# Two-direction recurrence beside conditioning products: later rank, a fourth weight tile, four column groups, and a substitution by halves

## Chip, core and metric

One NeuronCore of one Trainium2 chip runs the whole program in one launch. The metric is device microseconds (us) of that core; lower is better. Engines: PE (TensorE, matmuls), DVE (VectorE), ACT (ScalarE), POOL (GpSimd), SP (issues DMAs).

## What is computed

Two blocks, one after the other, on 512 tokens and 256 context tokens of width 1024. Block 1 mixes a two-direction RWKV recurrence with latent attention; block 2 has four attention layers. Each of the layers of both blocks is conditioned on a vector:

```python
mod   = silu(c)     @ ada_w[i] + ada_b[i]      # 1024 -> 3072, shift, scale, gate
mod_c = silu(c_ctx) @ ada_w[i] + ada_b[i]

def step(S, inp):                               # forward, and once more with reverse=True
    r_t, w_t, k_t, v_t, a_t, b_t = inp
    sa = einsum('bhij,bhj->bhi', S, a_t)
    S = S * w_t[..] + sa[..., None] * b_t[..] + v_t[..., None] * k_t[..]
    return S, einsum('bhij,bhj->bhi', S, r_t)
```

The four conditioning products of block 2 depend on nothing that block 1 computes.

## The kernel before

Block 1 does its projections and attention first (to about 480 us of the span). Then `rwkv` runs the recurrence in chunks of 64 tokens, two chunks to a **unit**, six units for each direction (d = 0 forward, d = 1 backward). For a unit, `rw_prep` builds the chunk matrices on all engines, and `rw_inv` inverts a triangular 64x64 matrix for each head and chunk. That goes through 16x16 diagonal blocks: they are carried to another layout by DMA through DRAM (tiles `dd`), solved on DVE by substitution (L1733 to L1735, 15 steps of one product and one reduction over all the columns before it, once for both directions), carried back, and put together to 64x64 with 32x32 matmuls (line L1750, tile `psi`). Then `rw_step` takes the state through two chunks (PE lines L1825 to L1848, tiles `psc`, `pss`), and adds to the result `y` (L1855). After the recurrence, `gnorm(0)` normalises the first pair of token tiles (PE L1540, DVE L1544 to L1577), the product with `w_out` follows, then `gnorm(1)`.

Beside the recurrence stands a generator, `fillers`. It emits the conditioning products of block 2, which `rwkv` draws a few pieces at a time (`self.fills`). `ada_steps` computes them: 4 layers x 3 thirds of 1024 columns; a third takes 16 weight tiles `adw` (128x512 f32, 256 KB each, loaded by L234 on the SP queue), each multiplied (L237) into the one PSUM tile `pad`; then the bias (L231, L240), the evacuation to an `adw` tile (L242, DVE) and stores to `mods` (L252). That is 192 weight tiles. The tiles `adw` come round robin out of a few buffers, so a load waits until the matmul that read the buffer last is through. `self.adj` is the number of column groups J: the 1024 columns of a third lie as J rows of 1024/J columns at partitions 0, 32, ... of `pad`, so one matmul has 1024/J columns and column group j of the array:

```python
nc.tensor.matmul(p[32 * j:32 * j + 32, 0:n], lhsT=sT[:, k, :], rhs=wt[:, c0:c0 + n], ...,
                 tile_position=(0, 32 * j))
```

Block 1's own conditioning at the start of the program (psw, 128x256) already has J = 4.

A scheduler sets the order of every engine's instructions at build time: by a rank, which is the place in the program unless `high_priority` moves it, and by its own estimate of when operands are there. An engine, and the DMA queue on SP, then takes its instructions strictly in that order. Unit 0's preparation and all of `rw_step` have high priority; the other pieces stand at their places.

Of the kernel before, what the change touches and what calls it, by code (L numbers as in the profile page):

```python
# [11 lines left out]
F32 = mybir.dt.float32  # L12
# [4 lines left out]
ALU = mybir.AluOpType  # L17
AX = mybir.AxisListType
# [1058 lines left out]
class Block1(Block2):  # L1077
# [371 lines left out]
    def rwkv(self, rp, adp):  # L1449
        nc, a = self.nc, self.a  # L1450
        big = [128, 4, 2, 128]
        self.slots(rp, [(f"{n}{q}", big, 2, F32) for q in range(2) for n in ("bt", "mb", "xa", "xb")])
        self.w2 = rp.tile([128, 512], F32, name="w2")
        self.a2 = rp.tile([128, 512], F32, name="a2")
        self.w0 = rp.tile([128, 2, 512], F32, name="w0")
        self.slots(rp, [("e", [128, 512], self.ebufs, F32), ("P", [128, 4, 2, 65], 2, F32), ("bk", big, 2, F32)])
        self.slots(rp, [("iv", [128, 16, 16], 3, F32)])
        for d in range(2):
            self.slots(rp, [(f"ih{d}", [128, 8, 32], 2, F32), (f"dg{d}", [128, 8, 16], 2, F32)])

        self.zd = [[rp.tile([128, 8, 32], F32, name=f"zd{d}{i}") for i in range(3)] for d in range(2)]
        for d in range(2):
            for t in self.zd[d]:
                nc.gpsimd.memset(t, 0.0)
        nc.sync.dma_start(out=self.w2, in_=a["rw_w2"][0].rearrange("d e f -> (d e) f"))
        nc.sync.dma_start(out=self.a2, in_=a["rw_a2"][0].rearrange("d e f -> (d e) f"))
        nc.sync.dma_start(out=self.w0, in_=a["rw_w0"][0].unsqueeze(0).to_broadcast([128, 2, 512]))
        nc.scalar.activation(out=self.wi, in_=self.wi, func=AF.Tanh)
        self.ha0 = rp.tile([128, 8], F32, name="ha0")
        nc.vector.tensor_scalar(self.ha0, self.a0c, 0.5, None, op0=ALU.mult)  # L1470
        self.hka = rp.tile([128, 2, 4], F32, name="hka")
        nc.vector.tensor_scalar(self.hka[:, 0], self.kac, 0.5, None, op0=ALU.mult)
        nc.vector.tensor_scalar(self.hka[:, 1], self.kac, -0.5, 1.0, op0=ALU.mult, op1=ALU.add)

        self.i32 = rp.tile([128, 32], F32, name="i32")
        nc.vector.tensor_reduce(out=self.i32, in_=self.ident.rearrange("p (b t) -> p t b", t=32), axis=AX.X, op=ALU.add)

        gl = self.gl
        for i, v in enumerate((a["rw_lnx_g"][0], a["rw_lnx_b"][0])):
            for h in range(2):  # L1480
                nc.sync.dma_start(out=gl[64 - 64 * h:128 - 64 * h, i], in_=v.rearrange("(a h v) -> h a v", h=2, v=64)[h].unsqueeze(0).to_broadcast([64, 4, 64]))
        nc.vector.tensor_scalar(gl, gl, 0.5, None, op0=ALU.mult)
        self.Rn = [None, None]
        self.psum(3, (("ad", 1), ("w", 3), ("c0", 1), ("c1", 1), ("iv0", 1), ("iv1", 1)))
        fill = iter(())
        if self.second:
            fill = self.fillers(adp)
        for i in range(6):
            us = [None, None]
            gens = [self.rw_prep(rp, i, d, us) for d in range(2)]  # L1490
            r = 0
            while gens:
                with self.tc.high_priority() if i < self.early_units else ExitStack():
                    gens = [g for g in gens if next(g, self) is not self]
                r += 1
                for _ in range(self.fills[i]):
                    next(fill, None)
            with self.tc.high_priority():
                for s in range(2):
                    for d in range(2):  # L1500
                        self.rw_step(rp, i, d, s, us[d])
        for _ in fill:
            pass

    early_units = 1

    def fillers(self, adp):

        b = self.second
        self.adj = 2  # L1510
        sT = self.ada_cond(adp, b["c"], b["c_ctx"], "ad")
        self.mds = []
        g = self.rpb_rows(adp, b["b_rpb"][0], ("adw", 3), "ad")
        self.rpb = next(g)
        yield from g
        for l in range(4):
            g = self.ada_steps(adp, sT, b["ada_w"][l], b["ada_b"][l], ("adw", 3), "ad")
            self.mds.append(next(g))
            yield from g

# [176 lines left out]
    def rw_inv(self, rp, d, mb):  # L1697


        nc = self.nc  # L1700
# [23 lines left out]
        U, Z, tmp = self.sub  # L1724
# [5 lines left out]
        yield  # L1730
        if d == 1:
            nc.vector.tensor_copy(U[hs], tmp[hs].rearrange("p s t -> p t s"))
            for n in range(1, 16):  # L1733
                nc.vector.tensor_tensor(out=tmp[:, 0:n, 0:n], in0=Z[:, 0:n, 0:n], in1=U[:, 0:n, n].unsqueeze(1).to_broadcast([128, n, n]), op=ALU.mult)
                nc.vector.tensor_reduce(out=Z[:, 0:n, n], in_=tmp[:, 0:n, 0:n], axis=AX.X, op=ALU.add)  # L1735
            nc.vector.tensor_copy(tmp, Z.rearrange("p s t -> p t s"))
        yield
        for k, src, dst, q in ((2, (tmp, Z)[d][hs], zt, nc.scalar), (1, (Z, tmp)[d][hs], zd, nc.sync)):
# [5 lines left out]
        def wp():  # L1744
            return self.ps.tile([128, 8, 32], F32, tag=f"iv{d}", bufs=1, name="psi")
# [8 lines left out]
        p = wp()  # L1754
# [4 lines left out]
        p = wp()  # L1759
# [7 lines left out]
        p = wp()  # L1767
# [10 lines left out]
        p = wp()  # L1778
# [6 lines left out]
        p = wp()  # L1785
# [203 lines left out]
```

## Time and profile before

| | |
|---|---|
| median of 3 runs | 3094.74 us (3083.89 to 3104.61) |
| profiled run: time, span of its execution | 3110.49 us, 3108.7 us |
| PE, DVE, ACT, POOL busy over the span | 90%, 58%, 44%, 40% |
| recurrence with conditioning beside it | about 480 to 1022 us of the span |

Times of rows are us from the start of the span; a group's mean is in ns. A matmul of f32 leaves two records, so "x2" on L237 is one matmul; a few records are missing. PEclk is the granted share of the 2.4 GHz clock: 1.00 is 2.4 GHz, 0.50 is 1.2 GHz, and what lies between is a mean over a stretch. SPq rows are DMA issues on SP's queue. A busy PE is one with a matmul in flight, not one at its peak.

### The profile page before, as it was taken

To read this page: it belongs to the slowest core of one execution; us is meant where nothing else is said; L and a number is where in the kernel's file an instruction comes from. 1 tells how busy PE (TensorE), PEld (TensorE's weight loads), DVE (VectorE), ACT (ScalarE), POOL (GpSimd) and SP (SyncE) were. 2 spreads that over 40 slices of the span, in tenths; PEclk is the share of its full clock that TensorE was granted. 3 is DMA by queue.
4 is the path that set the end of the run, shared out by engine and by line. 5 is a ranking of instruction groups with operands and counts; after the bars stand their busy time and mean duration, and the time that the engine had idled before them with its cause. 6 is when DMAs were issued, how large, how long until landed. Compare 5 with 4: busy or idle time off the path is not lost.

```text
span 3108.7 us, 56171 instructions
## 1 busy us (share of the span) xinstructions
PE 2800.7 (90%) x21983; PEld 2409.1 (77%) x21983; DVE 1789.0 (58%) x3470; ACT 1364.3 (44%) x2940; POOL 1256.5 (40%) x1348
## 2 busy tenths in 40 slices
PE   6989987999999689998969999996999898789998
PEld 4978875555645688987969999886999797778878
DVE  3345534655454745667554655545677787556785
ACT  3435523322221344557434555534445354345673
POOL 3313344443321452534534554562432344334454
PEclk8999996998778689999989999998999999899999
DMA  5252144444344331011122111223111121221112
GB/s 186 59 157 73 51 138 127 118 118 115 93 115 123 126 94 42 28 39 45 44 88 63 52 45 54 65 81 89 55 38 32 42 66 53 62 80 57 48 35 72
DMA packets 252692, 238.40 MB, mean 77 GB/s; under 512 B 59218, under 2 KB 217859, under 8 KB 252427
## 3 DMA queue, kind: packets, MB, share of 16 engines
q1 hardware_dynamic: 217712, 217.48, 23.9%
q10 hardware_dynamic: 33770, 16.29, 1.8%
q8 instruction: 173, 2.83, 0.4%
q0 software_dynamic: 944, 1.05, 0.2%
q14 instruction: 93, 0.75, 0.1%
HBM read 207.15 MB, written 28.07 MB: 76 GB/s over the span
## 4 chain that ended last, share of the span: by engine, by line
PE 66%; DVE 16%; DMA 6%; issue 4%; ACT 4%; POOL 2%; SPq 0%; ACTq 0%; DVEq 0%; POOLq 0%
PE psw L187 10%; PE psw L188 10%; PE psw L189 10%; PE psp L567 5%; PE pad L237 4%; PE psi L1750 3%; PE ps L544 3%; PE ps L545 2%; PE pso L559 2%; PE psp L187 2%; PE psp L189 2%; PE psp L188 2%; PE psw L1659 2%; DMA gbc<-mods 1%; DMA adw<-in_ada_w_dram 1%
## 5 line engine op out<-in xcount | busy, mean ns | idle before, releaser
L180 POOL TENSOR_TENSOR wl<-wr,wh 128x512 fp32r<-128x512 f32 x362 | 481.8, 1346 | 556.3 <-ACT wh L373 442.4
L187 PE MATMUL psw<-wh,hh 128*128 128x256 f32 x2152 | 625.4, 291 | 43.0 <-DVE yt L697 33.7
L189 PE MATMUL psw<-wh,hl 128*128 128x256 f32 x2152 | 615.3, 286 | 1.9 <-POOL hl L180 1.8
L188 PE MATMUL psw<-wl,hh 128*128 128x256 f32 x2152 | 616.2, 286 | 0.3 <-POOL wl L180 0.3
L187 PEld LDWEIGHTS psw<-wh,hh 128*128 128x128 f32 x2152 | 413.6, 192 | 54.5 <-DVE yt L697 36.8
L189 PEld LDWEIGHTS psw<-wh,hl 128*128 128x128 f32 x2152 | 413.6, 192 | 2.9 <-POOL hl L180 2.7
L188 PEld LDWEIGHTS psw<-wl,hh 128*128 128x128 f32 x2152 | 414.0, 192 | 0.8 <-POOL wl L180 0.5
L527 DVE TENSOR_REDUCE nm<-ps 128x1 f32<-128x768 f32 (+2 forms) x384 | 293.3, 774 | 153.5 <-PE ps L545 122.0
L373 ACT CAST wh<-wr 128x512 fp32r<-128x512 f32 x362 | 221.7, 617 | 269.5 <-PE psw L189 123.0
L528 ACT ACTIVATE P<-ps,nm 128x768 f32<-128x768 f32 (+1 forms) x288 | 247.0, 859 | 170.9 <-DVE nm L527 151.9
L535 DVE TENSOR_TENSOR ptl<-psp,pth 128x512 fp32r<-128x512 f32 x360 | 244.1, 685 | 131.9 <-ACT pth L534 129.6
L534 ACT CAST pth<-psp 128x512 fp32r<-128x512 f32 x360 | 207.3, 588 | 145.0 <-PE psp L567 118.2
L187 PE MATMUL psw<-hh,wh 128*128 128x512 f32 (+1 forms) x640 | 230.6, 360 | 21.5 <-DVE z L405 15.4
L567 PE MATMUL psp<-ident,P 128*128 128x128 f32 x1408 | 219.3, 274 | 7.8 <-DVE P L1023 6.9
L188 PE MATMUL psw<-hl,wh 128*128 128x512 f32 (+1 forms) x640 | 225.9, 353 | 0.0
L189 PE MATMUL psw<-hh,wl 128*128 128x512 f32 (+1 forms) x640 | 225.7, 353 | 0.2 <-POOL wl L180 0.2
L544 PE MATMUL ps<-kh,qs 128*128 128x512 f32 (+1 forms) x608 | 203.6, 341 | 17.9 <-ACT P L528 11.3
L237 PE MATMUL pad<-adw,ad_s 128*32 128x512 f32 x384 | 200.6, 700 | 14.8 <-DMA adw<-in_ada_w_dram 11.3
L545 PE MATMUL ps<-kz,qs 128*128 128x512 f32 (+1 forms) x608 | 183.3, 320 | 0.0
L567 PEld LDWEIGHTS psp<-ident,P 128*128 128x128 f32 x1408 | 164.8, 141 | 10.6 <-DVE P L1023 6.8
L187 PEld LDWEIGHTS psw<-hh,wh 128*128 128x128 f32 x640 | 121.8, 190 | 42.3 <-DVE z L405 19.5
L183 POOL TENSOR_SCALAR u<-ot 64x512 f32<-64x512 f32 x88 | 50.9, 578 | 252.9 <-ACT ot L585 249.4
(490 smaller groups left out, 6307.0 us busy)
## 6 DMA issues: line engine op xcount, KB each, us to landing
adw<-in_ada_w_dram SPq DMA_DIRECT2D x240, 256.0 KB
wr<-in_a_w_in_dram SPq DMA_DIRECT2D x80, 256.0 KB
wr<-in_b_w_in_dram SPq DMA_DIRECT2D x64, 256.0 KB
wr<-in_c_w_in_dram SPq DMA_DIRECT2D x64, 256.0 KB
wr<-in_w_in_dram SPq DMA_DIRECT2D x52, 256.0 KB
gbc<-mods SPq DMA_DIRECT2D x72, 128.0 KB
xscr<-xt SPq DMA_DIRECT2D x36, 256.0 KB
wr<-in_a_w_out_dram SPq DMA_DIRECT2D x32, 256.0 KB
```

What stands on the lines that cost most here:

```text
L180: self.nc.gpsimd.tensor_tensor(out=out, in0=in0, in1=in1, op=op)
L187: mm(out, lhsT=ah, rhs=bh, start=start, stop=False)
L188: mm(out, lhsT=ah, rhs=bl, start=False, stop=False)
L189: mm(out, lhsT=al, rhs=bh, start=False, stop=stop)
L237: nc.tensor.matmul(p[32 * j:32 * j + 32, 0:n], lhsT=sT[:, k, :], rhs=wt[:, c0:c0 + n], start=(k == 0), stop=False, tile_position=(0, 32 * j))
L373: nc.scalar.copy(out=h, in_=raw)
L527: nc.vector.tensor_reduce(out=nm, in_=S, axis=AX.X, op=ALU.max, negate=True)
L528: nc.scalar.activation(out=dst, in_=S, func=AF.Exp, bias=nm, accum_out=l)
L535: nc.vector.tensor_tensor(out=lo[:, 0:n], in0=p[:, 0:n], in1=h[:, 0:n], op=ALU.subtract)
L544: mm(out[:, c0:c0 + n], lhsT=qs, rhs=kh[:, k0:k0 + n], start=True, stop=False)
L545: mm(out[:, c0:c0 + n], lhsT=qs, rhs=kl[:, k0:k0 + n], start=False, stop=True)
L567: self.nc.tensor.transpose(p[:, 256 * i + 128 * t:256 * i + 128 * t + 128], P[t][:, c0 + 128 * kt:c0 + 128 * kt + 128], self.ident)
```

## The change

Three edits, all beside or inside the recurrence. The conditioning pieces are emitted under a rank 2000 places later; their tiles have four buffers in place of three, and four column groups in place of two (a weight tile is then read by two matmuls of 256 columns on two column groups in place of one of 512). The substitution solves both 8x8 diagonal blocks of each 16x16 block at once in 7 steps, and gets the off-diagonal 8x8 block as a product of three matrices, in four DVE instructions of 512 products or sums.

```diff
@@ rwkv
-                for _ in range(self.fills[i]):
-                    next(fill, None)
+                with self.tc.high_priority(offset=-self.later):
+                    for _ in range(self.fills[i]):
+                        next(fill, None)
-    early_units = 1
+    early_units, later = 1, 2000
@@ fillers
-        self.adj = 2
+        self.adj = 4
-        g = self.rpb_rows(adp, b["b_rpb"][0], ("adw", 3), "ad")
+        g = self.rpb_rows(adp, b["b_rpb"][0], ("adw", 4), "ad")
-            g = self.ada_steps(adp, sT, b["ada_w"][l], b["ada_b"][l], ("adw", 3), "ad")
+            g = self.ada_steps(adp, sT, b["ada_w"][l], b["ada_b"][l], ("adw", 4), "ad")
@@ rw_inv
-            for n in range(1, 16):
-                nc.vector.tensor_tensor(out=tmp[:, 0:n, 0:n], in0=Z[:, 0:n, 0:n], in1=U[:, 0:n, n].unsqueeze(1).to_broadcast([128, n, n]), op=ALU.mult)
-                nc.vector.tensor_reduce(out=Z[:, 0:n, n], in_=tmp[:, 0:n, 0:n], axis=AX.X, op=ALU.add)
+            for n in range(1, 8):
+                un = bass.AP(tensor=U.tensor, offset=sub(U, 0, n, 1, 1).offset, ap=[U.ap[0], [136, 2], [0, n], [16, n]])
+                nc.vector.tensor_tensor(out=sub(tmp, 0, 0, n, n), in0=sub(Z, 0, 0, n, n), in1=un, op=ALU.mult)
+                nc.vector.tensor_reduce(out=sub(Z, 0, n, n, 1).rearrange("p h i j -> p h (i j)"), in_=sub(tmp, 0, 0, n, n), axis=AX.X, op=ALU.add)
+            nc.vector.tensor_tensor(out=big, in0=z1.unsqueeze(2).to_broadcast(b8), in1=u12.unsqueeze(1).to_broadcast(b8), op=ALU.mult)
+            nc.vector.tensor_reduce(out=mid, in_=big, axis=AX.X, op=ALU.add)
+            nc.vector.tensor_tensor(out=big, in0=mid.unsqueeze(2).to_broadcast(b8), in1=z2.rearrange("p k l -> p l k").unsqueeze(1).to_broadcast(b8), op=ALU.mult)
+            nc.vector.tensor_reduce(out=Z[:, 0:8, 8:16], in_=big, axis=AX.X, op=ALU.add)
```

(`sub` views both diagonal halves; `big` is a new tile of 128x512.) Lines behind the edits stand later in the changed file: L1750 is L1766 there, L1825 to L1855 are L1841 to L1871, L1540 is L1541.

PE inside the inversion of the last unit (`psi` are the 32x32 matmuls of the inversion, `pad` the conditioning). Before:

```order
L1750 MATMUL psi<-zd_4645,zd_4646 32x32 x32
L1750 MATMUL psi<-zd_4648,zd_4649 32x32 x17
L237 MATMUL pad<-adw,ad_s 32x512
L1750 MATMUL psi<-zd_4648,zd_4649 32x32 x12
L237 MATMUL pad<-adw,ad_s 32x512
L1750 MATMUL psi<-zd_4648,zd_4649 32x32 x3
L1750 MATMUL psi<-zd_4644,H 32x32
L237 MATMUL pad<-adw,ad_s 32x512
L1750 MATMUL psi<-zd_4644,H 32x32 x11
L237 MATMUL pad<-adw,ad_s 32x512
```

The same place in the changed kernel:

```order
L1766 MATMUL psi<-zd_4646,zd_4647 32x32 x32
L1766 MATMUL psi<-zd_4649,zd_4650 32x32 x32
L1766 MATMUL psi<-zd_4645,H 32x32 x32
L1766 MATMUL psi<-zd_4648,H 32x32 x32
L237 MATMUL pad<-adw,ad_s 32x256 x3
L1766 MATMUL psi<-H,zd_4645 32x32 x16
L237 MATMUL pad<-adw,ad_s 32x256 x2
L1766 MATMUL psi<-H,zd_4648 32x32 x16
L237 MATMUL pad<-adw,ad_s 32x256 x4
L1766 MATMUL psi<-tt,mb 32x32 x16
```

A conditioning matmul now stands between whole groups of the inversion. From the first unit to the last step, the order before has 140 runs of L237 with all 192 tiles; the changed order has 71 runs with 128 tiles.

PE at the end of the recurrence (L1848 and L1864 are the last products of a step, L240 the bias, L1540 and L1541 the first matmuls of `gnorm(0)`). Before:

```order
L237 MATMUL pad<-adw,ad_s 32x512
L240 MATMUL pad<-adw,ad_7536 32x512 x2
L1750 MATMUL psi<-tt,mb 32x32 x8
L1750 MATMUL psi<-mb,hb 32x32 x16
L1750 MATMUL psi<-tt,mb 32x32 x8
L1835 MATMUL pss<-xs,mb 64x64 x8
L1750 MATMUL psi<-mb,hb 32x32 x16
L1848 MATMUL psc<-R,mb 64x64
L1842 MATMUL pss<-R,bt 64x64 x8
L1848 MATMUL psc<-R,mb 64x64 x7
L1835 MATMUL pss<-xs,mb 64x64 x8
L263 MATMUL psw<-ident,md_r 128x40
```

In the changed kernel:

```order
L1864 MATMUL psc<-R,mb 64x64 x7
L240 MATMUL pad<-adw,ad_6888 32x256
L237 MATMUL pad<-adw,ad_s 32x256 x32
L240 MATMUL pad<-adw,ad_6888 32x256 x4
L237 MATMUL pad<-adw,ad_s 32x256 x32
L240 MATMUL pad<-adw,ad_7684 32x256 x4
L237 MATMUL pad<-adw,ad_s 32x256 x32
L240 MATMUL pad<-adw,ad_7684 32x256 x4
L237 MATMUL pad<-adw,ad_s 32x256 x32
L240 MATMUL pad<-adw,ad_7684 32x256 x4
L263 MATMUL psw<-ident,md_r 128x40
L1541 MATMUL psw<-ident,bon 64x8 x8
```

Four whole thirds, 64 weight tiles, stand behind the last step and ahead of `gnorm(0)`.

DVE at that place in the changed kernel (L1871 adds the last results to `y`, L242 evacuates `pad`, L1545 on is `gnorm(0)`):

```order
L1843 COPY xs<-psc 64x256 x2
L1853 COPY R<-pss 64x4x64 x2
L1871 TENSOR_TENSOR y_4590<-y_4590,psc 64x256 x4
L242 COPY adw<-pad 128x256 x5
L265 COPY md_m<-psw 128x40
L613 TENSOR_REDUCE ms<-ssq 128x2
L268 SCALAR_TENSOR_TENSOR md_A<-md_m 128x8 x2
L614 TENSOR_SCALAR ms<-ms 128x2
L1545 TENSOR_SCALAR bv<-psw 64x16 x2
L1556 TENSOR_REDUCE m<-y_4589 128x16
```

In the order before, the first rows of `gnorm(0)` stood ahead of the last three pairs of these additions to `y`. On SP, too, the loads that `gnorm(0)` and the product with `w_out` use (`zt`, `wr`) now stand behind all 192 loads of `adw`.

## Rows read from the trace of the kernel before

**Rows 1.** Busy time of each engine by stretch, clock and DMA.

```profile
core 0: us, PE busy (x) PEld busy (x) DVE busy (x) ACT busy (x) POOL busy (x), PEclk, DMA share, GB/s
620.00:710.00 90.00, 83.33 (x886) 45.92 (x885) 50.57 (x119) 22.88 (x60) 39.99 (x51) 0.91 0.45 121
980.00:1022.00 42.00, 41.59 (x548) 23.17 (x545) 3.94 (x9) 9.54 (x27) 0.00 (x0) 0.70 0.41 122
1022.00:1052.00 30.00, 23.31 (x248) 21.25 (x245) 26.18 (x48) 10.60 (x24) 15.13 (x11) 0.62 0.62 208
480.00:1022.00 542.00, 510.06 (x5191) 302.27 (x5190) 286.26 (x648) 140.68 (x367) 172.15 (x211) 0.84 0.42 113
480.00:530.00 50.00, 43.22 (x196) 35.66 (x196) 24.82 (x56) 16.67 (x38) 16.82 (x20) 0.61 0.31 84
```

**Rows 2.** The chain that ended last, 480 to 1022 us, shares by line.

```profile
by line: PE pad L237 23.9%; PE psi L1750 17.5%; PE psw L1659 8.8%; DVE t L1734 5.6%; DMA adw<-in_ada_w_dram 4.8%; DVE Z L1735 2.7%; PE psc L1825 2.1%; DMA dd<-dg 1.9%; issue 1.7%; DMA t<-dd 1.7%; DMA rpt<-rpbb 1.6%; PE pad L871 1.6%; PE pss
```

**Rows 3.** 480 to 1022 us, single lines: L237, L240, then DVE L1734, L1735.

```profile
480.00:1022.00 542.00, 200.57 (x384) 25.61 (x384) 0.84 0.42 113
480.00:1022.00 542.00, 14.31 (x48) 1.76 (x48) 0.84 0.42 113
480.00:1022.00 542.00, 38.71 (x90) 0.84 0.42 113
480.00:1022.00 542.00, 21.51 (x90) 0.84 0.42 113
```

**Rows 4.** PE in order of time: conditioning matmuls, 512 and 256 columns.

```profile
540.62 1.04 PE L237 MATMUL pad<-adw,ad_s 128*32 128x512 f32 x2 [0.46 <-DMA adw<-in_ada_w_dram]
710.23 1.92 PE L237 MATMUL pad<-adw,ad_s 128*32 128x512 f32 x2
707.38 1.92 PE L237 MATMUL pad<-adw,ad_s 128*32 128x512 f32 x4
42.34 0.63 PE L237 MATMUL psw<-adw,ad_s 128*32 128x256 f32 x4
33.47 1.07 PE L237 MATMUL psw<-adw,ad_s 128*32 128x256 f32 x4
40.26 1.50 PE L237 MATMUL psw<-adw,ad_s 128*32 128x256 f32 x24
```

**Rows 5.** DVE groups by form, 480 to 1022 us.

```profile
L1668 DVE TENSOR_TENSOR x<-psw,cm 64x512 f32<-64x512 f32 x40 | 27.5, 688 | 51.1 <-PE psw L1659 50.5
L1734 DVE TENSOR_TENSOR t<-Z,U 128x100 f32<-128x100 f32 x6 | 2.6, 436 | 0.2
L1734 DVE TENSOR_TENSOR t<-Z,U 128x9 f32<-128x9 f32 x6 | 1.2, 204 | 0.1
L1735 DVE TENSOR_REDUCE Z<-t 128x10 f32<-128x100 f32 x6 | 1.6, 258 | 0.2
L1735 DVE TENSOR_REDUCE Z<-t 128x2 f32<-128x4 f32 x6 | 0.9, 157 | 0.2
```

**Rows 6.** SP's queue in order of time: twelve loads with three buffers.

```profile
532.44 15.32 SPq L234 DMA_DIRECT2D adw<-in_ada_w_dram  x12
```

**Rows 7.** Stretches of block 1's own conditioning; columns as in rows 1.

```profile
15.00:20.00 5.00, 3.50 (x18) 0.69 (x16) 0.00 (x0) 1.40 (x6) 0.00 (x0) 1.00 1.02 351
30.00:35.00 5.00, 2.15 (x8) 1.01 (x9) 3.09 (x19) 0.61 (x4) 0.00 (x0) 0.50 0.94 297
```

**Rows 8.** PE and DVE in order of time, last steps beside `gnorm(0)`.

```profile
1022.34 1.47 PE L1540 MATMUL psw<-ident,bon 8*64 8x8 f32 x16
1023.74 2.40 PE L1825 MATMUL psc<-R,x 128*128 128x64 f32 x10
1035.13 2.39 PE L1825 MATMUL psc<-R,x 128*128 128x64 f32 x10
...
1029.83 0.86 DVE L1845 TENSOR_TENSOR R<-pss,sn 64x256 f32<-64x256 f32 x2
1049.86 0.85 DVE L1855 TENSOR_TENSOR y<-y,psc 64x256 f32<-64x256 f32 x2
1061.64 0.36 DVE L1544 TENSOR_SCALAR bv<-pad 64x16 f32<-64x16 f32 x2
```

More of the change, by code (lines that the diff above doesn't have):

```diff
@@ L1456, in rwkv @@
         self.slots(rp, [("e", [128, 512], self.ebufs, F32), ("P", [128, 4, 2, 65], 2, F32), ("bk", big, 2, F32)])
-        self.slots(rp, [("iv", [128, 16, 16], 3, F32)])
+        self.slots(rp, [("iv", [128, 16, 16], 3, F32), ("iw", [128, 8, 8, 8], 1, F32)])
         for d in range(2):
@@ L1732, in rw_inv, with sub @@
             nc.vector.tensor_copy(U[hs], tmp[hs].rearrange("p s t -> p t s"))
-            for n in range(1, 16):
-                nc.vector.tensor_tensor(out=tmp[:, 0:n, 0:n], in0=Z[:, 0:n, 0:n], in1=U[:, 0:n, n].unsqueeze(1).to_broadcast([128, n, n]), op=ALU.mult)
-                nc.vector.tensor_reduce(out=Z[:, 0:n, n], in_=tmp[:, 0:n, 0:n], axis=AX.X, op=ALU.add)
+            def sub(x, i, j, ni, nj, both=True):
+                v = x.rearrange("p s t -> p (s t)")[:, 16 * i + j:]
+                return bass.AP(tensor=v.tensor, offset=v.offset, ap=[v.ap[0]] + [[136, 2]] * both + [[16, ni], [1, nj]])
+            for n in range(1, 8):
+                un = bass.AP(tensor=U.tensor, offset=sub(U, 0, n, 1, 1).offset, ap=[U.ap[0], [136, 2], [0, n], [16, n]])
+                nc.vector.tensor_tensor(out=sub(tmp, 0, 0, n, n), in0=sub(Z, 0, 0, n, n), in1=un, op=ALU.mult)
+                nc.vector.tensor_reduce(out=sub(Z, 0, n, n, 1).rearrange("p h i j -> p h (i j)"), in_=sub(tmp, 0, 0, n, n), axis=AX.X, op=ALU.add)
+            z1, z2 = Z[:, 0:8, 0:8], Z[:, 8:16, 8:16]
+            u12 = U[:, 0:8, 8:16].rearrange("p j k -> p k j")
+            big, mid = [rp.tile([128, 8, 8, 8], F32, tag="iw", bufs=1, name="iw"), U[:, 0:8, 0:8]]
+            b8 = [128, 8, 8, 8]
+            nc.vector.tensor_tensor(out=big, in0=z1.unsqueeze(2).to_broadcast(b8), in1=u12.unsqueeze(1).to_broadcast(b8), op=ALU.mult)
+            nc.vector.tensor_reduce(out=mid, in_=big, axis=AX.X, op=ALU.add)
+            nc.vector.tensor_tensor(out=big, in0=mid.unsqueeze(2).to_broadcast(b8), in1=z2.rearrange("p k l -> p l k").unsqueeze(1).to_broadcast(b8), op=ALU.mult)
+            nc.vector.tensor_reduce(out=Z[:, 0:8, 8:16], in_=big, axis=AX.X, op=ALU.add)
             nc.vector.tensor_copy(tmp, Z.rearrange("p s t -> p t s"))
```

## Prediction, made before the changed kernel ran

> **What bounds the kernel now.** I read first the busy times by stretch. From 480 to 1022 us, where the change acts, PE has a matmul in flight for 510 of 542 us (94%), DVE is busy 286, ACT 141, POOL 172 [rows 1]. Then the chain of waits of that stretch: its largest part, 24%, is the conditioning matmul L237, 4.8% more is PE waiting for a weight tile, 17.5% are the 32x32 matmuls of the inversion, and the substitution (L1734, L1735) has 8.3% [rows 2]. So the recurrence is held by PE's strict order: work that the recurrence does not need stands ahead of work that it does. Third, single lines: the conditioning holds PE for 200.6 us and its biases for 14.3 us; everything else in the stretch holds it for 510.1 - 214.9 = 295 us [rows 1, 3].
>
> **What the column groups do.** A weight tile alone costs 1.04 us at 2.4 GHz and 1.92 us at 1.2 GHz as one matmul of 512 columns; two tiles on both column groups cost the same 1.92 us. As two matmuls of 256 columns a tile costs 0.63 or 1.07 us, and twelve such matmuls in a row took 1.50 us, so four groups do run at once [rows 4]. Call a pass what can run at once. By the order before, 140 runs make 155 passes, 200.6 / 155 = 1.29 us each, between the two clocks. In the changed order the recurrence keeps 128 tiles in 71 runs, which are 92 passes. A pass shrinks to 0.63/1.04 = 61% or 1.07/1.92 = 56%; I take 58%, 0.75 us, so 69 us. The biases go from 14.3 us for twelve thirds to 8/12 of that at 60%, 6 us. The added weight loads (twice as many, 25.6 us now [rows 3]) lie beside matmuls. PE then has 295 + 69 + 6 = 370 us of work in the recurrence, 140 less.
>
> **What the gaps give back.** Conditioning also fills PE's waits, and with less of it gaps open: DMA round trips of the inversion and DVE work then show. Now 6% of the stretch is idle. Two stretches without conditioning matmuls give the other bound: 14% at 480 to 530 us, 22% at 1022 to 1052 us [rows 1]. Some filling remains (128 tiles), so I take 15%: 370 / 0.85 = 435 us, a gain of 107 us. At 6% the gain is 148, at 22% it is 68.
>
> **The substitution.** Now (38.7 + 21.5) / 6 = 10.0 us a unit [rows 3]. After: seven products of up to 98 elements, between 0.20 and 0.44 us, say 2.0 us together; seven reductions between 0.16 and 0.26 us, 1.4 us; four instructions of 512 elements, for which the nearest row is 0.69 us, 2.8 us [rows 5]. Together 6.2 us, 3.8 us less a unit, 23 us in all. DVE is no bound (about 263 of 435 us). This shortens a link between DMA round trips and narrows the gaps; I do not add it to the 107 us, it is part of why I take 15% and not 20%.
>
> **What the later rank costs.** The changed order has 64 tiles, four thirds, behind the last step. Nothing hides them: on PE they stand ahead of the first matmul of `gnorm(0)`, on DVE their evacuations stand ahead of its reductions, on SP their loads stand ahead of `zt` and `wr`. The pace is that of the loads. With three buffers twelve issues took 15.32 us, (15.32 - 0.33) / 11 = 1.36 us each [rows 6], so a buffer comes round in 4.09 us, of which the matmul held it 1.04 and the load with its semaphores 3.05. With four buffers and 0.63 us it comes round in 3.68 us, 0.92 us a tile; that asks for 285 GB/s, and 351 was moved at 15 to 20 us [rows 7]. Between two thirds the pipeline empties: the next third's first load takes the buffer of the bias tile, so it waits for the last weight matmul (0.63 us) and the bias matmuls (about 0.6), and lands 3.05 us on; the sixteenth tile follows four cycles later. That is 4.3 + 4 x 3.68 = 19 us a third, 76 us for four. At 1.2 GHz it is 1.07 + 1.0 + 3.05 + 4 x 4.12 = 21.6, so 86 us. At 15 to 20 us, with PE in waits for the same loads 30% of the time, 2.4 GHz was granted; at 30 to 35 us, after a longer pause, 1.2 [rows 7]. A third has one pause of 4 us, so I take 80 us. Five loads of together 4 MB (X, rows) also move ahead of the last 72 tiles; at 351 GB/s they cost up to 12 us, so the bound above is 98, the bound below 70. The Trainium skill ("TensorE: Matmul & The Clock Gate", section "Loop structure matters more than you think") says that a DMA wait between every two matmuls leaves PE at the low clock. By that rule it would be the 86 us; the stretch at 15 to 20 us does not bear it out.
>
> **The rest.** Before, `gnorm(0)` began at 1022.3 us with two half steps still to do, which ran beside it [rows 8]; alone they take about 12 us of PE and DVE work (estimate from the step matmuls of 2.40, 2.39 us and the links between them) and now lie ahead: +12. In return `gnorm(0)` is not interrupted by their DVE work (0.86 us, three times 0.85, five copies of about 0.4: 5.5 us up to 1061 us [rows 8]): -5. A transpose of `md_r` ahead of `gnorm(0)` on PE must wait for a load that is issued after the last store: about +3, by the 3.05 us above.
>
> **Sum.** -107 + 80 + 12 + 3 - 5 = -17 us. The trace is of a run of 3110.5 us, 0.5% above the median of the three timed runs, 3094.7; there the sum gives 3078 us.
>
> **Rivals.** About 1%, 31 us, is what a measurement of this kernel can tell from no change.
> 1. *The gaps do not open.* Pieces of low rank still fill every wait, and half as many runs break up the inversion. At 6% idle: 148 gained, -58 us, 3037 us. It is over 1% faster from a gain of 121 us on, that is, under 12% idle. For it: only 32 us are idle now. Against: both stretches without conditioning lie above. Chance 0.32, with a shorter tail counted in.
> 2. *The clock falls* (the slower side). The clock was 0.91 at 620 to 710 us but 0.70 at 980 to 1022 us, where PE had only inversion and conditioning, and 0.61 at 480 to 530 us [rows 1]. If the recurrence is granted 0.70 in place of 0.84, its work on PE is 370 x 0.84/0.70 = 444 us; with 10% idle (a slower PE hides more) 493 us, a gain of 49: +41 us, 3136 us. It decides below a clock of 0.715. Against: the mean of 0.84 held although most conditioning runs of before used one column group at a time. Chance 0.25, with idle shares over 23% at the old clock, which end there too.
> 3. *PE is not the bound.* Its 94% is time in flight; if waits on DMA and DVE hold the recurrence, idle time goes to the 22% of rows 1: 68 gained, +22 us, 3117 us, within 1%. Chance 0.15. The Trainium skill ("Perfetto Trace Analysis", "Identifying the Most-Contended Engine") judges PE by its weight loads and not by matmul busy time; by that PE is at 302/542 = 56%, which speaks for this case.
> 4. *The column groups do not run at once.* Then 128 tiles cost 134 us, PE has 295 + 134 + 10 = 439 us, and with 10% idle the recurrence takes 488: 54 gained, +36 us, 3131 us. The 1.50 us row excludes it nearly; chance 0.02, counted in the slower side.
>
> **How the numbers follow.** The forecast case (idle 12 to 20%) has 0.28, with rival 3 the time stays within 1% with 0.43; faster 0.32, slower 0.25. Predicted: 3078 us, for the likeliest case alone 3064 to 3105. The range for 8 in 10 reaches to rival 1 and rival 2: 3035 to 3135.
>
> **What would show it.** Right: between the last `y` addition and the first `gnorm(0)` matmul PE does nothing but L237 and L240 for 70 to 98 us, with a tile every 0.9 to 1.05 us and a pause at each third; the recurrence ends near 480 + 435 + 12 = 927 us; its PE idle share is 12 to 20% and its conditioning takes some 75 us of PE; the substitution takes about 6 us a unit. Wrong: an idle share near 6% or over 23%; a clock under 0.72 in the recurrence; a tail paced at over 1.3 us a tile; anything but shifted times after the second `gnorm`.

## The result, and the profile after

The changed kernel takes 3119.62 us (median of 8 runs, 3108.74 to 3133.86), the kernel before 3094.61 us beside it (8 runs, 3083.89 to 3104.61): a ratio of 1.0072, interval 1.0051 to 1.0093. It is slower by 0.7%, where 0.5% faster was forecast (3078 us); the time lies inside the forecast range, the change on the other side of zero. The profiled run took 3119.93 us (span 3118.1), so it is a typical one; the profiled run of before, at 3110.5 us, lay 16 us above its kernel's median and above all 8 of these runs. The profiles differ by 9.4 us where the medians differ by 25.

The stretches after, with columns as in [rows 1]: the recurrence with conditioning beside it, four pieces of the tail and the whole of it, and three pieces from the start of the recurrence.

```profile
480.00:937.00 457.00, 419.97 (x5452) 330.56 (x5450) 281.11 (x584) 143.73 (x379) 178.15 (x207) 0.75 0.37 103
...
937.00:957.00 20.00, 13.82 (x63) 2.94 (x64) 0.83 (x3) 0.00 (x0) 0.00 (x0) 0.52 0.66 196
957.00:980.00 23.00, 15.51 (x76) 3.17 (x74) 0.42 (x1) 0.00 (x0) 0.74 (x2) 0.57 0.64 190
980.00:1003.00 23.00, 15.13 (x74) 3.19 (x72) 0.42 (x1) 0.00 (x0) 0.00 (x0) 0.50 0.59 183
1003.00:1026.00 23.00, 16.54 (x84) 3.41 (x80) 0.42 (x1) 0.00 (x0) 0.00 (x0) 0.50 0.59 183
...
937.50:1031.30 93.80, 61.66 (x290) 12.93 (x290) 2.04 (x6) 0.00 (x0) 0.74 (x2) 0.52 0.59 178
...
480.00:530.00 50.00, 45.09 (x220) 35.72 (x218) 29.07 (x64) 17.51 (x41) 16.25 (x20) 0.65 0.38 103
530.00:620.00 90.00, 81.87 (x1074) 60.99 (x1073) 50.30 (x96) 29.44 (x80) 41.77 (x46) 0.68 0.38 102
620.00:710.00 90.00, 84.01 (x1217) 69.71 (x1216) 62.77 (x124) 28.82 (x78) 37.72 (x43) 0.77 0.32 90
```

The recurrence ended at 937 us, near the forecast 927, but by another way: PE was busy for 420 of 457 us, 8% idle and not 15%, and its clock was 0.75, not 0.84. From 620 to 710 us it was 0.77 where it had been 0.91 [rows 1]. In the tail PE did conditioning alone, at a clock of 0.50 to 0.57.

Single lines of the same stretch, 480 to 937 us (the columns for the line's engine, then clock and DMA): the conditioning (L237), its biases (L240), and the 32x32 matmuls of the inversion (now L1766), as in [rows 3].

```profile
480.00:937.00 457.00, 70.96 (x512) 17.84 (x512) 0.75 0.37 103
480.00:937.00 457.00, 9.00 (x64) 2.11 (x64) 0.75 0.37 103
480.00:937.00 457.00, 112.33 (x2688) 108.00 (x2688) 0.75 0.37 103
```

The 128 weight tiles that stayed cost 71.0 us (69 forecast) and the biases 9.0 (6). So conditioning shrank as forecast, and everything else grew: 420.0 - 80.0 = 340 us where the forecast kept 295.

SP's queue in the tail, in order of time: the four stores of each third (L252) and the loads behind them.

```profile
937.87 1.15 SPq L252 DMA_DIRECT2D mods<-adw  x4
...
959.43 1.15 SPq L252 DMA_DIRECT2D mods<-adw  x4
960.63 12.09 SPq L234 DMA_DIRECT2D adw<-in_ada_w_dram  x12
...
981.95 1.15 SPq L252 DMA_DIRECT2D mods<-adw  x4
...
1005.05 1.15 SPq L252 DMA_DIRECT2D mods<-adw  x4
...
1027.09 1.15 SPq L252 DMA_DIRECT2D mods<-adw  x4
```

From store to store a third takes 21.6, 22.5, 23.1 and 22.0 us, for 16 tiles.

PE at the end of the tail, in order of time (in brackets what it waited for, us).

```profile
1025.49 1.08 PE L240 MATMUL pad<-adw,ad 1*32 1x256 f32 x8
1031.04 0.30 PE L263 MATMUL psw<-ident,md_r 40*128 40x40 f32 x1 [4.47 <-DMA md_r<-in_norm_g_dram]
1031.27 1.47 PE L1541 MATMUL psw<-ident,bon 8*64 8x8 f32 x16
```

`gnorm(0)` begins at 1031.3 us; before, at 1022.3 [rows 8]. The last `y` addition ends at 937.5, so 93.8 us lie between. `gnorm(1)` is counted below from the last of its first 16 matmuls (L1541): 1061.7 us, before 1060.7.

### The profile page after: what moved, and what is told of

Its sections match the earlier page's. It is cut to its first block, busy times and chain, and to the rows that moved or that the text cites. A ratio compares the mean times of both kernels' runs of the same rounds, so it can differ in the third digit from the quotient of the medians.

```text
span 3118.1 us, 56987 instructions
## 1 busy us (share of the span) xinstructions
PE 2760.4 (89%) x22415; PEld 2439.5 (78%) x22415; DVE 1781.9 (57%) x3398; ACT 1362.1 (44%) x2940; POOL 1263.5 (41%) x1348
## 4 chain that ended last, share of the span: by engine, by line
PE 63%; DVE 15%; DMA 8%; ACT 4%; issue 4%; POOL 3%; SPq 0%; ACTq 0%; DVEq 0%; POOLq 0%
PE psw L187 10%; PE psw L188 9%; PE psw L189 9%; PE psp L567 5%; PE psi L1766 3%; DMA adw<-in_ada_w_dram 3%; PE ps L544 3%; PE ps L545 2%; PE psw L1660 2%; PE pso L559 2%; PE psp L187 2%; PE psp L189 2%; PE pad L237 2%; PE psp L188 2%; DMA gbc<-mods 1%
## 5 line engine op out<-in xcount | busy, mean ns | idle before, releaser
L187 PEld LDWEIGHTS psw<-wh,hh 128*128 128x128 f32 x2152 | 412.2, 192 | 53.4 <-DVE yt L697 36.5
L237 PE MATMUL pad<-adw,ad_s 128*32 128x256 f32 x768 | 128.3, 517 | 40.9 <-DMA adw<-in_ada_w_dram 38.5
```

The source lines that it names most:

```text
L187: mm(out, lhsT=ah, rhs=bh, start=start, stop=False)
```

## The experiments

In every run the recurrence is measured from the first matmul of the first unit's preparation on PE (464 to 469 us) to the last `y` addition. "Conditioning" and "other" are the times in which PE had a matmul of that kind in flight, worked out from all PE records there (both can be in flight at once, so their sum exceeds PE's busy time; this "other" is more than the difference 340 above). The expectations count conditioning loosely: the 384 tiles of some are the matmuls of 256 columns, 192 weight tiles in all, of which 64 stand in the changed kernel's tail; the 314 given there for its recurrence are 256 by the trace. Recurrence, clock and the times of work come from one profiled run each; "off" is how far that run lies from its kernel's median.

| kernel | median us | off us | ratio to before, interval | recurrence us | conditioning us | other us | clock | other x clock |
|---|---|---|---|---|---|---|---|---|
| before | 3090.7 to 3095.0 | +16 | | 581.6 | 214.0 | 347.3 | .819 | 284 |
| after | 3119.62 | 0 | 1.0072, 1.0051 to 1.0093 | 471.8 | 79.6 | 361.9 | .745 | 270 |
| e1 rank alone | 3170.54 | +10 | 1.0269, 1.0231 to 1.0308 | 507.4 | 126.4 | 343.8 | .789 | 271 |
| e2 groups, tiles alone | 3078.16 | +4 | 0.9969, 0.9948 to 0.9990 | 548.9 | 129.3 | 374.5 | .740 | 277 |
| e3 substitution alone | 3105.50 | -10 | 1.0061, 1.0027 to 1.0094 | 552.3 | 204.2 | 332.3 | .868 | 288 |
| e4 all but the rank | 3092.61 | +13 | 1.0016, 0.9995 to 1.0036 | 573.0 | 142.2 | 391.0 | .704 | 275 |
| e6 rank 600 | 3092.19 | -4 | 0.9985, 0.9966 to 1.0004 | 526.0 | 139.4 | 364.4 | .726 | 265 |
| e9 as e4, done twice | 3103.57 | 0 | 1.0035, 1.0016 to 1.0055 | 573.3 | 190.2 | 350.9 | .824 | 289 |
| e10 as after, done twice | 3151.59 | +4 | 1.0187, 1.0162 to 1.0212 | 483.2 | 116.2 | 337.6 | .790 | 267 |
| g600 as e2, rank 600 | 3086.80 | +6 | 0.9965, 0.9942 to 0.9988 | 540.5 | 135.0 | 363.6 | .746 | 271 |
| e8 half the conditioning | 3002.09 | +1 | 0.9702, 0.9666 to 0.9737 | 475.4 | 61.3 | 369.7 | .723 | 267 |
| g300 as e2, rank 300 | 3074.31 | 0 | 0.9943, 0.9923 to 0.9962 | 549.6 | 130.5 | 384.8 | .712 | 274 |
| r300 rank 300 | 3079.35 | +3 | 0.9963, 0.9939 to 0.9988 | 555.2 | 140.3 | 383.2 | .725 | 278 |

The last column is the point: PE's other work, counted at full clock, changes less (265 to 289 us) than its time does (332 to 391 us), and the order of the times is nearly that of the clocks. The clock does not go by the conditioning time alone: e1's 126 us had .789, e4's 142 us .704.

### The three edits apart

**e1, the rank alone** (before, with the pieces drawn under `high_priority(offset=-2000)`).

> The kernel before with the later rank (2000) alone; two column groups, three tiles and the substitution of 15 steps stay. Its order leaves 69 of the 192 tiles behind the last step. Theory A (what the later rank moves behind the recurrence is paid there in full, at the pace of the loads): with three buffers a third takes about 28 us, so some 115 to 125 us of unhidden conditioning, against 60 to 100 us gained in the recurrence: slower by 20 to 60 us, 3115 to 3155. Theory B (the rank helps, and one of the other edits spoils it): faster than 3095.

Windows of the recurrence and of the tail.

```profile
464.00:972.00 508.00, 458.30 (x5181) 318.18 (x5182) 294.68 (x659) 147.54 (x384) 182.61 (x228) 0.79 0.35 97
...
972.00:1086.00 114.00, 79.29 (x154) 10.79 (x154) 2.73 (x4) 0.00 (x0) 0.74 (x2) 0.85 0.51 155
```

1.0269: 68 tiles start behind the last `y` addition, 114 us of conditioning alone and 119.5 us up to `gnorm(0)`. The recurrence is shorter by 74 us, so the rank alone loses. That is 15 us above A's range, with the mechanism and the tail that A named (115 to 125 us); B falls.

**e2, four column groups and four tiles alone.**

```diff
-        self.adj = 2
+        self.adj = 4
-            ... ("adw", 3), "ad")      # two such lines
+            ... ("adw", 4), "ad")
```

> The kernel before with four column groups and four tiles alone, at the old rank: all 192 tiles stand beside the recurrence, in 118 runs. Theory A: conditioning holds PE for about 100 us in place of 201 and part of that comes back: faster by 30 to 70 us, 3025 to 3065. Theory B (thinner conditioning lets the clock fall, and the recurrence pays it back): within 15 us of 3095, with a granted clock under 0.78 from 480 us to the end of the recurrence.

The recurrence, and L237 in it.

```profile
466.00:1015.00 549.00, 485.77 (x5859) 354.13 (x5859) 313.02 (x695) 152.21 (x392) 198.77 (x239) 0.74 0.45 126
466.00:1015.00 549.00, 118.07 (x768) 27.68 (x768) 0.74 0.45 126
```

L237 gives up 82 of its 200.6 us, and 12.5 us of the whole remain by the medians (between the profiles the recurrence is 33 us shorter, but that of before lies 16 us above its median): the clock is 0.74, the other work takes 27 us more, idle time 63 us in place of 44. A falls. B, which had the clock take the gain, is nearly met: 16.8 us below 3095, where it allowed 15.

**e3, the new substitution alone.**

> The kernel before with the substitution by halves alone. Theory A: 10.0 us a unit become about 7 us (four instructions of 512 elements cost more than the 0.69 us of the prediction); part of some 18 us on DVE comes back: faster by 0 to 18 us, 3077 to 3095. Theory B (the substitution is hidden behind PE, which is full of conditioning): no change, 3090 to 3100.

```profile
467.00:1019.00 552.00, 513.41 (x5353) 309.76 (x5353) 286.48 (x604) 151.07 (x390) 189.00 (x234) 0.87 0.45 124
```

DVE has 286 us where it had 313, and the time is not less but 0.6% more. Six of its 12 runs took 3088 to 3100 us at a mean clock of .942 to .948, like those of before, and six 3111 to 3130 us at .930 to .938; why half were granted less stays open. Its profile is of a run of 3095.1 us, in the faster half, and shows a recurrence 27 to 29 us shorter than in the two profiles of before (the second is e5, below), which lie above theirs: read without the runs beside it, it would have been taken for a gain. Nor is all of that a gain in the profile: `gnorm(1)` begins 23 us behind the last `y` addition, in before 10. Neither reading foresaw a loss.

**e4, all but the rank** (`high_priority(offset=-self.later)` taken out again).

> The changed kernel with the rank taken back (all pieces at their places in the program), the rest as changed: no tile stands behind the last step. Theory A: the unhidden stretch of 94 us is gone, the recurrence keeps most of its gain: 3000 to 3045. Theory B (the rank gains and groups, tiles or substitution lose): 3120 or more.

```profile
469.00:1042.00 573.00, 511.87 (x5858) 369.44 (x5859) 302.17 (x622) 151.93 (x392) 200.09 (x239) 0.70 0.43 121
469.00:1042.00 573.00, 133.19 (x768) 29.82 (x768) 0.70 0.43 121
```

3092.61: no gain to be measured, with a clock of 0.70 (the profiled run is the slowest of the 12; their mean clocks are .911 to .921, those of before .933 to .949). Neither reading held. Without a tail nothing is lost, and the three other edits together buy nothing. Up to here the clock only goes along with the conditioning; the next runs ask whether it follows it.

### Does the clock follow the conditioning?

**e9, e4 with every conditioning matmul issued twice on halved inputs.**

Against e4, in part:

```diff
-            nc.vector.tensor_scalar(sT[:, :, r], ..., 0.5, None, op0=ALU.mult)
+            nc.vector.tensor_scalar(sT[:, :, r], ..., 0.5 if ptag is None else 0.25, None, op0=ALU.mult)
+                    for again in range(1 if ptag is None else 2):
                         for j in range(J // 2 * jh, J // 2 * jh + J // 2):
```

> The changed kernel without the rank, with each conditioning matmul of the filler issued twice on halved inputs (the same sum). There conditioning held PE 142 us at a clock of .704, 100 us at full clock; other PE work 391 us, 275 at full clock. A (PE's clock falls because conditioning holds the array for less time): the clock comes back to .78 to .86, other PE work falls to 320 to 355 us, conditioning takes 235 to 260, recurrence 600 to 640 us, time 3115 to 3160. B (the clock has nothing to do with the conditioning's thickness): other PE work stays at 380 to 400, conditioning 270 to 290, recurrence 690 to 730, time 3205 to 3250.

The recurrence and its conditioning line (here L238), then the 32x32 matmuls of the inversion (here L1767).

```profile
465.00:1038.00 573.00, 520.00 (x6626) 372.81 (x6627) 301.08 (x622) 152.83 (x392) 199.21 (x239) 0.82 0.43 121
465.00:1038.00 573.00, 182.35 (x1536) 69.57 (x1536) 0.82 0.43 121
...
469.00:1048.00 579.00, 102.87 (x2688) 95.15 (x2688) 0.83 0.42 120
```

The 32x32 matmuls in e4:

```profile
469.00:1048.00 579.00, 126.78 (x2688) 117.20 (x2688) 0.71 0.43 121
```

384 more matmuls, and the recurrence is 573 us in both profiles; that of e4 is of a run 13 us above its median, that of e9 of one at its median, so the medians are the safer measure: 11 us slower, not over 100. The clock rose from 0.70 to 0.82, and the untouched inversion, 2688 records in both, fell from 126.8 to 102.9 us. That is not a matter of one profile: over all runs the mean clock is .929 to .940 in e9 and .911 to .921 in e4. At the old clock the doubled work would have been some 142 us more than e4 had (an estimate: its own conditioning once more), with only 61 us of PE idle to put it in. A holds for the clock and the other work; its conditioning (190 us, 235 to 260 expected), recurrence (600 to 640) and time (3115 to 3160) came out lower. B falls. So with the same tiles and loads the clock follows what conditioning puts on the array, and a part of what is saved in PE time is paid back through it. Whether halved inputs alone move the clock was not tested.

**e10, the changed kernel with the same doubling.**

> The changed kernel with each conditioning matmul of the filler issued twice on halved inputs (the same sum); about 81 tiles stand behind the last step. A (clock by how long conditioning holds PE, in the recurrence; the tail is paced by its weight loads, 1.34 us per tile): recurrence clock .79 to .85 where it was .745, other PE work 325 to 350 us where it was 362, tail about 105 to 115 us, time 3150 to 3180. B (the clock is not moved by it, and the tail is paced by PE at half clock: 57 us doubled): recurrence clock .72 to .76, other PE work 355 to 370, tail 130 to 145 us, time 3200 to 3235.

Windows of its recurrence, then of its tail.

```profile
468.00:952.00 484.00, 443.22 (x5856) 338.09 (x5856) 278.75 (x586) 146.75 (x384) 186.31 (x228) 0.79 0.34 95
...
952.00:975.00 23.00, 16.15 (x146) 6.32 (x140) 0.85 (x2) 0.00 (x0) 0.00 (x0) 1.00 0.62 191
975.00:1000.00 25.00, 16.70 (x152) 6.97 (x151) 0.42 (x1) 0.00 (x0) 0.74 (x2) 1.00 0.62 191
...
952.00:1058.00 106.00, 76.71 (x676) 31.69 (x670) 2.12 (x5) 0.00 (x0) 0.74 (x2) 0.98 0.64 198
```

In the recurrence the clock rose, 0.745 to 0.790, less than in e9, and it became 11 us longer. In the tail it went from 0.52 to 0.98, with twice the matmuls between the same waits for loads, and the tail's 80 tiles took 112 us, 1.3 us each without the load of `md_r` where it was 1.4. A's numbers hold. That the pace stayed does not settle what the half clock cost: twice the matmuls at twice the clock hold a buffer as long as before (L238's 74.4 us for 80 tiles, 0.93 each; after, 57.4 us for 64, 0.90). A doubled tail at half the clock did not occur.

**e8, the changed kernel without the conditioning of layers 2 and 3**, which use that of layers 0 and 1; that part of the computation is left out.

> The changed kernel that leaves out the conditioning of layers 2 and 3 (they use that of 0 and 1), so 192 tiles in place of 384 and no tail. Conditioning would hold PE some 49 us of the recurrence where it held 79.6. A (the clock pays back what conditioning gives up): other PE work rises from 362 to 372 to 400 us, clock .68 to .73, recurrence 460 to 480 us, no shorter than with the 314 tiles of the changed kernel (471.8); time 2995 to 3020, by the tail alone. B (the clock stays at .745): recurrence 435 to 447, time 2960 to 2985.

```profile
466.00:941.00 475.00, 420.74 (x5419) 340.28 (x5420) 300.59 (x616) 150.88 (x392) 202.66 (x238) 0.72 0.34 93
...
850.00:941.00 91.00, 71.04 (x1101) 65.52 (x1100) 52.06 (x121) 24.97 (x64) 29.72 (x31) 0.63 0.29 87
```

96 tiles in the recurrence in place of 128, 18 us less conditioning, and it is no shorter (475.4 us, after 471.8). The clock is 0.72, and 0.63 from 850 us on, behind the last weight tile. The whole is 118 us faster than the changed kernel: the tail of 94 us is gone, and `gnorm(0)` begins 27 us inside the recurrence. A holds but for the other work, 370 us, which is just below its 372; B, 435 to 447 us, falls.

### The rank without a tail

**e6** (`later = 600` in place of 2000), **g600** (the same without the new substitution), **g300** (the same at 300) and **r300** (the changed kernel at 300).

> The changed kernel with the rank at 600 in place of 2000, so that all but about two of the conditioning tiles stand ahead of the last recurrent step and no tail is left. A (the loss is the unhidden tail of 94 us at half clock, and the rest is a thinner conditioning paid back by the clock): the tail is gone, all 384 tiles run inside the recurrence as in the changed kernel without the rank (3092.6), recurrence 555 to 580 us at a clock of .70 to .76, time 3075 to 3100. B (a late rank costs by itself, by the order of the work, also without a tail): 3110 or more.

> The kernel before with four column groups, four weight tiles and the rank at 600, without the new substitution. A (without a tail the rank moves nothing of size, since what the thinner conditioning gives back goes to the clock): within 12 us of the same kernel without the rank (3078), recurrence clock .70 to .78. B (a later rank spreads the tiles into steps with spare PE time): 3065 or less.

> Four column groups, four weight tiles and the rank at 300, without the new substitution: conditioning ends a little ahead of the recurrence, so that the first layer norm's tables (30 us apart from the second's) are done inside it. At rank 0 the recurrence ended at 1014.6 and the second table at 1021.3; at rank 600 the recurrence at 1006.2 and the second table only at 1034.8. A (rank gives some 8 us of recurrence and the tables' place the other 28): recurrence ends at 1000 to 1010, second table at 1008 to 1018, time 3060 to 3075. B (the clock gives it back): within 8 us of the kernel without a rank, 3070 to 3086.

> The changed kernel with its rank at 300 in place of 2000: the four column groups, the weight tiles and the new substitution stay, no tile is left behind the last step, and both norm tables are made inside the recurrence. Beside the same kernel without the new substitution (3074.31) this prices the substitution where the clock is lowest. A (the DVE time that it saves is no PE time, and what it brings forward the clock gives back): 3078 to 3094, recurrence clock .69 to .73, no faster than without it. B (the 26 us of DVE time shorten the recurrence once the tail is gone): 3050 to 3070.

The recurrence of e6, of g600, of g300 and of r300, in this order.

```profile
466.00:992.00 526.00, 482.91 (x5756) 345.01 (x5756) 283.67 (x591) 146.99 (x384) 187.98 (x229) 0.73 0.45 126
```

```profile
466.00:1006.00 540.00, 480.58 (x5785) 345.69 (x5783) 294.68 (x672) 147.02 (x384) 183.25 (x230) 0.75 0.44 125
```

```profile
464.00:1014.00 550.00, 498.95 (x5855) 364.06 (x5856) 308.29 (x695) 152.85 (x392) 195.63 (x240) 0.71 0.44 126
```

```profile
465.00:1020.00 555.00, 504.31 (x5852) 360.02 (x5853) 302.22 (x622) 151.94 (x392) 200.59 (x240) 0.72 0.44 125
```

At 600 the tail is gone, and with it 27 us of the time. e6's recurrence (526 us) is shorter than its A had it (555 to 580), but conditioning ends with the recurrence, so hardly anything hides the two `gnorm`: `gnorm(1)` begins 38 us after the last `y` addition, in g600 29 us, in g300 and r300 only 7 us. What the shorter recurrence brings is spent there. Both A hold in time. In g300 both `gnorm` begin about when they do in e2 (1020.7 us for the second, 1021.3 in e2), later than A had it; the time lies in both ranges, so its readings are not told apart, and its interval overlaps that of e2. r300's A holds. The changed kernel is thus 40 us faster with a rank of 300 than with 2000, and g300, 0.6% below before, beats both kernels. Between 300 and 600 the intervals overlap in both pairs, so that hiding the `gnorm` gains time is argued from the profiles, not shown.

The substitution costs or changes nothing in each of four pairs: +15 us in e3 (medians 3105.5 and 3090.7 beside it), +14 from e2 to e4, +5 from g600 to e6, +5 from g300 to r300; the intervals of the last two pairs overlap. It never gained, though half of e3's runs took what before takes. Part of it is seen in e3 and e6: `gnorm(1)` stands 13 and 10 us further behind the last `y` addition than without it. The rest is not settled by these runs.

**e5, the kernel before again**, for a profile at a typical time.

> The kernel before again, for a second profile. The first was of its slowest run (clock .933, 3110 us). A (a run's time goes with PE's granted clock, and the difference between runs lies in the recurrence): at a time near the median of 3091 to 3095 the recurrence is 560 to 572 us long at a clock of .83 to .86 (581.6 at .819 in the first profile), and what follows it is 2046 to 2060 us as before. B (the runs differ in block 1): recurrence 579 to 584, the rest shorter by 12 to 20.

```profile
468.00:1048.00 580.00, 533.72 (x5437) 326.78 (x5438) 313.34 (x696) 152.47 (x393) 195.18 (x239) 0.83 0.44 120
```

The profiled run was again above the median (3107.3 us, median of 8 runs 3090.29), so the question was not answered. It shows that the profile repeats: 579.7 us at .827, 581.6 at .819. The other times say more. Of 29 runs of before that stood beside e1 to e4, the fastest, 3074.2 us, had a mean granted clock of .946, the slowest, 3103.7, had .933, and over all of them the correlation of time and clock is -0.86. Which of the two drives the other, a correlation does not say.

## Why the prediction was wrong

By its own steps, from the two profiles:

| step | forecast us | measured us |
|---|---|---|
| recurrence and the half steps ahead of the old `gnorm(0)` (-107, +12) | -95 | -84.8 (937.5 - 1022.3) |
| tail and the load of `md_r` (+80, +3) | +83 | +93.8 |
| `gnorm(0)` not interrupted | -5 | -8.0 (38.4 to 30.4) |
| from `gnorm(1)` to the end | 0 | +8.4 |
| sum, profile to profile | -17 | +9.4 |
| the profiled run of before above its kernel's median | | +16 |

The rows ahead of the sum miss by 10, 11, -3 and 8 us. Without the first or the second miss the sum would be about -1, not -17, so no single one explains the difference; the clock is the one where the mechanism was wrong and not a size alone.

- **The step that failed is the clock held at 0.84.** "Everything else in the stretch holds it for 295 us" was carried over unchanged, and 295 x 0.84 / 0.75 is 330; it was 340, with the half steps in it that the sum kept apart as +12. That is rival 2's mechanism, half way along: it had 0.70 and 444 us of PE work, and the trace shows 0.75 and 420. The argument against it, that the mean of 0.84 held although most runs of conditioning used one column group at a time, looked at the wrong thing: the change took conditioning out of the stretch (in flight for 214 us of the recurrence before, 80 after), and the clock was .819 and .745. The rows to look at were the windows without conditioning, 0.61 at 480 to 530 us and 0.62 at 1022 to 1052 [rows 1]. Rival 2 names the first, but the sum used both for their idle share alone. That fewer conditioning matmuls lower the clock is shown by e9 against e4, in the other direction; what exactly the clock answers to is not.
- **The idle share failed the other way**: 8%, not 15%. A slower PE hides more, as rival 2 said. 50 us more PE work (420 for 370) and 28 us less idle time (37 for 65) make the stretch 22 us longer than 435; 12 of these were in the sum, so the recurrence ended only 10 us late. That it came so near is two errors of opposite sign, which is luck.
- **Conditioning's own size was right**: 71.0 us for 69, 9.0 for 6. Four column groups do run at once; rival 4, which had 134 us, is out.
- **The tail was mis-sized**: 22.3 us a third (89.2 / 4) where 21.6 had been worked out for 1.2 GHz and 19 for 2.4, and 80 us chosen between 76 and 86. PE was at 1.2 GHz for nearly all of it. The pace, 1.4 us a tile, is over the 1.3 that the prediction itself took as a sign of being wrong. The Trainium skill ("TensorE: Matmul & The Clock Gate", section "Loop structure matters more than you think") has a long DMA wait between every two matmuls keep PE at the low clock. The tail was granted it (0.50 to 0.57), but with waits of 0.3 to 1.5 us ahead of a tile in its second third, which are hardly the long ones meant; the prediction left the word "long" out. e10's tail waits for the same loads and was granted 0.98, e1's, with one matmul of 512 columns a tile, 0.85, so the waits alone do not decide. The load of `md_r` cost 4.5 us, not 3.
- **The substitution** takes (11.33 + 8.22) / 6 = 3.3 us a unit for the steps and 3.9 for the four large instructions, 7.1 in all; 6.2 was forecast, 10.0 stood before. DVE groups after, 480 to 937 us, and the two lines of the steps:

```profile
L1750 DVE TENSOR_TENSOR iw<-U,Z 128x512 f32<-128x512 f32 x6 | 8.1, 1350 | 0.2
L1748 DVE TENSOR_TENSOR iw<-Z,U 128x512 f32<-128x512 f32 x6 | 7.0, 1172 | 0.2
L1749 DVE TENSOR_REDUCE U<-iw 128x64 f32<-128x512 f32 x6 | 4.1, 681 | 0.1
...
480.00:937.00 457.00, 11.33 (x42) 0.75 0.37 103
...
480.00:937.00 457.00, 8.22 (x42) 0.75 0.37 103
```

  The reductions of 512 elements cost what [rows 5] had for 512 (0.68 us); the products with two broadcast operands cost 1.17 and 1.35 us, which no row of before had. That it would narrow the gaps brought no time (e3).
- **Unforeseen**: from `gnorm(1)` to the end it is 8.4 us longer. In the profiles of the other variants that is 2051 to 2059 us, in the two of before 2047 and 2048. 5.4 us of it lie inside `gnorm(1)`: its transposes on PE begin 17.6 us behind its start in both profiles of before, and 23.0 us in every variant. Before and after:

```profile
1078.29 3.68 PE L1576 MATMUL psw<-ident,y 64*64 64x64 f32 x64 [17.39 <-DVE y L1570]
...
1084.68 3.57 PE L1577 MATMUL psw<-ident,y 64*64 64x64 f32 x62 [17.86 <-DVE y L1571]
```

  So the -8.0 and the +8.4 belong together. From the start of `gnorm(0)` to these transposes it is 55.9 us before and 53.4 after, 2.5 us gained where 5 were forecast. From there to the end it is 2030.4 and 2033.4 us, 3 us more, in a stretch that takes 2028 to 2036 us in the other profiles; a cause of their own is not shown for them.
- **The base**: the sum of one profile was taken off the median of the runs, as if a run 16 us above the median had nothing to do with the stretch in question.

So the balance was right in kind, a shorter recurrence against an unhidden tail, and each side was off by about 10 us to the bad. The tail decides it: with the rank at 0, 600 or 300 the same kernel is 27, 27 and 40 us faster than with 2000 (e4, e6, r300), and the rank alone loses 2.7% (e1). But without the tail there is no gain of size either: e4 took what before takes. Rival 3's time, 3117 us, is nearly the measured one, by luck: it had 22% idle. It is not shown as a cause: DVE's 26 us less brought nothing, and PE's idle share was 7 to 12% in all profiles.

## What to carry to other kernels

PE time that filler matmuls take was not a plain gain to remove here, where the clock was below 1.00: before counting such a gain, compare the granted clock in windows with and without the filler, and cost the remaining work at the lower one too. Move filler late only as far as it still ends inside the work that hides it; the profiles suggest, far enough ahead that what follows (here both `gnorm`) is hidden too. Place a profiled run among the times of its own kernel before its microseconds go into a sum.

## What the runs showed of the hardware

- The granted clock lay below 1.00 in a recurrence with PE busy nine tenths of the time. With 214 us of it holding conditioning it was .819, with 80 us .745; with e4's 142 us .704, and with the same tiles done twice .824. In e8 it was 0.63 behind the last weight tile, with PE busy for 71 of 91 us, mostly with steps and 32x32 matmuls. How a matmul's shape enters was not measured.
- Additional conditioning matmuls cost far less than their own time: 384 more, in flight for 142 us when done once, made the kernel 11 us slower by the medians (e4, e9). In e10 the recurrence grew from 471.8 to 483.2 us.
- A tail of loads with a wait ahead of nearly each tile ran at a mean clock of 0.52 with one pass over a tile and at 0.98 with two, with DMA at 178 and 198 GB/s.
